# An elementwise add and GELU on one core: row-blocked arrays in place of column slices

## The chip, the core and the metric

The kernel runs on one core of one Trainium2 chip. The metric is the device time of one execution in microseconds (us), as the median of several runs. Beside the runs there is one profiled execution, whose span is the time from its first to its last instruction.

## The reference

```python
x, y: float32 arrays of 1024 x 4096            # 16.78 MB each
z = x + y
out = 0.5 * z * (1 + tanh(sqrt(2 / pi) * (z + 0.044715 * z ** 3)))   # float32
```

Every element of the output depends on the same element of x and of y alone, so the 4,194,304 elements may be handled in any order and any grouping. 33.55 MB are read and 16.78 MB are written.

## The kernel before

**Layout.** Each array is seen as 128 partitions of 32,768 float32 values ("columns" below). Partition p holds 8 consecutive rows of the array, 128 KB in HBM. A load or a store takes a range of columns, so it moves 128 stretches whose starts lie 128 KB apart.

**Buffers.** The tile `zt` (128 x 32768) receives x, then holds the sum z, then the result. y goes through two buffers of 8192 columns. The scratch tiles `wt[c]` lie in PSUM, two of them (`PS = 2`), 2048 columns each.

**Work.** The columns are cut into 16 chunks of 2048. Each chunk c has four steps:

- `add(c)` (L149): z = x + y, in place in `zt`. It runs on DVE for chunks 0, 2, 4, 6, 8 and 12 (`by_dve`), and on POOL for the others.
- `mag(c)` (L154): ACT writes |z| to the PSUM scratch. Because there are two scratch tiles, it needs `end(c - 2)`.
- `gelu(c)` (L157): ACT computes the tanh form of GELU of -|z|, in place in the scratch.
- `end(c)` (L166): DVE adds max(z, 0) to the scratch and writes the result over z.

**Order.** Four queues are written out by hand, and each engine works through its own in order. POOL has its adds in order of chunks, ACT has mag and gelu of each chunk in order, and DVE has all ends in order, with its adds put in between: `by_dve = {0: 0, 2: 0, ...}` says that the add of chunk 2 stands ahead of `end(0)`, and so on. SyncE (SP) issues all transfers, on one queue: y0 (8192 columns), x0 (16384), y1 (8192), x1 (16384), y2, y3 (8192 each), and the stores of 16384, 10240 and 6144 columns. SP waits, in its order, for what a transfer needs: y2 and y3 for the adds that free their buffer, a store for the ends of its columns. The first store waits in addition for the first half of `end(8)` (`FIRST = 8`), so that it joins the queue as the last load nears its end. The functions `begin_early` and `wait_late` move the first two transfers ahead of the program's opening barrier and the last wait behind its closing one; neither is changed.

Of the kernel before, what the change touches and what calls it, by code (L numbers as in the profile page):

```python
# [8 lines left out]
def begin_early(nc, count):  # L9


    head, body = (b.instructions for b in nc.main_func.blocks[:2])
    SP = mybir.EngineType.SP
    moved = [i for i in body if i.engine == SP and isinstance(i, mybir.InstDMACopy)][:count]
    assert not any(i.sync_info and i.sync_info.on_wait for i in moved)
    assert all(i.regs_accessed() == ((), ()) for i in moved)
    at = next(k for k, i in enumerate(head) if i.engine == SP)
    for k, i in enumerate(moved):
        body.remove(i)
        head.insert(at + k, i)  # L20


def wait_late(nc):

    body, end = (b.instructions for b in nc.main_func.blocks[1:3])
    last = [i for i in body if isinstance(i, mybir.InstDMACopy)][-1]
    (sem,) = [u.id for u in last.sync_info.on_update]
    all_done = end[0]  # L30
    reset = next(i for i in end if isinstance(i, mybir.InstDrain) and i.is_reset_sema)
    at = end.index(reset)
    clear = end[at + 1]
    first, stop = reset.reset_range_start, reset.reset_range_stop
    assert all_done.engine == mybir.EngineType.SP and reset.engine == mybir.EngineType.Pool
    assert isinstance(clear, mybir.InstISA) and clear.engine == mybir.EngineType.Pool
    waits = all_done.sync_info.on_wait
    (its,) = [w for w in waits if w.id == sem]

    end[0] = mybir.InstDrain(  # L40
        name=all_done.name, engine=all_done.engine, debug=all_done.debug, is_reset_sema=False,
        sync_info=mybir.SyncInfo(on_wait=[w for w in waits if w.id != sem], on_update=[]),
    )
    parts = []
    for f, e in ((first, sem), (sem + 1, stop)):
        if f < e:
            nc.gpsimd.sem_clear(range(f, e))
            parts.append(nc.cur_bb.bb.instructions.pop())
    end[at + 1 : at + 2] = parts
    end.append(  # L50
        mybir.InstEventSemaphore(
            name=clear.name, engine=mybir.EngineType.Activation, debug=clear.debug,
            sync_info=mybir.SyncInfo(
                on_wait=[its],
                on_update=[
                    mybir.SyncUpdate(
                        sync_type="semaphore", id=sem, ant_name=its.ant_name,
                        update_mode="sem-sub-imm", update_value=its.wait_value,
                    )
                ],  # L60
            ),
        )
    )


@with_exitstack
def kernel(
    ctx: ExitStack,
    tc: tile.TileContext,
    x: bass.AP,  # L70
    y: bass.AP,
    out: bass.AP,
):

    nc = tc.nc
    P = nc.NUM_PARTITIONS
    fp32 = mybir.dt.float32
    act = mybir.ActivationFunctionType
    alu = mybir.AluOpType

    N, D = x.shape
    assert N % P == 0
    TOT = N // P * D  # L90
    xv, yv, ov = (a.rearrange("(p n) d -> p (n d)", p=P) for a in (x, y, out))

    YS = 8192
    CH = 2048
    PS = 2
    xloads = [16384, 16384]
    yloads = [8192, 8192, 8192, 8192]
    FIRST = 8
    stores = [16384, 10240, 6144]

    def ranges(sizes):
        ends = [sum(sizes[: i + 1]) for i in range(len(sizes))]
        assert ends[-1] == TOT
        return [(e - f, e) for e, f in zip(ends, sizes)]

    xr, yr, sr, cr = (ranges(r) for r in (xloads, yloads, stores, [CH] * (TOT // CH)))
    C = len(cr)

    by_dve = {0: 0, 2: 0, 4: 2, 6: 4, 8: 8, 12: 10}

    def over(rs, lo, hi):
        return [i for i, (a, b) in enumerate(rs) if a < hi and b > lo]

    pool_sb = ctx.enter_context(tc.tile_pool(name="xz", bufs=1))
    pool_y = ctx.enter_context(tc.tile_pool(name="y", bufs=2))
    pool_w = ctx.enter_context(
        tc.tile_pool(name="w", bufs=PS, space=bass.MemoryType.PSUM)
    )

    zt = pool_sb.tile([P, TOT], fp32, tag="z", name="z")  # L120
    yt, wt, ends = {}, {}, {}

    def load_x(i):
        a, b = xr[i]
        nc.sync.dma_start(out=zt[:, a:b], in_=xv[:, a:b])

    def load_y(i):
        a, b = yr[i]
        s, o = divmod(a, YS)
        if o == 0:  # L130
            yt[s] = pool_y.tile([P, YS], fp32, tag="y", name=f"y{s}")
        nc.sync.dma_start(out=yt[s][:, o : o + b - a], in_=yv[:, a:b])  # L132

    def store(i):
        a, b = sr[i]
        ins = nc.sync.dma_start(out=ov[:, a:b], in_=zt[:, a:b])
        if i == 0:
            tc.add_manual_dep(
                ins.ins,
                ends[FIRST].name,  # L140
                mybir.DependencyInfo(mybir.DependencyClass.Sync, mybir.DependencyReason.DATA),
                reason="the stores join the queue when the last load is nearly done",
            )

    def add(c):
        a, b = cr[c]
        s, o = divmod(a, YS)
        eng = nc.vector if c in by_dve else nc.gpsimd
        eng.tensor_add(out=zt[:, a:b], in0=zt[:, a:b], in1=yt[s][:, o : o + b - a])  # L149

    def mag(c):
        a, b = cr[c]
        wt[c] = pool_w.tile([P, CH], fp32, tag="w", name=f"w{c}")
        nc.scalar.activation(out=wt[c], in_=zt[:, a:b], func=act.Abs)  # L154

    def gelu(c):
        nc.scalar.activation(  # L157
            out=wt[c], in_=wt[c], func=act.Gelu_apprx_tanh, scale=-1.0
        )

    def end(c):
        a, b = cr[c]
        parts = 2 if c == FIRST else 1
        n = (b - a) // parts
        for o in range(0, b - a, n):
            ins = nc.vector.scalar_tensor_tensor(  # L166
                out=zt[:, a + o : a + o + n], in0=zt[:, a + o : a + o + n], scalar=0.0,
                in1=wt[c][:, o : o + n], op0=alu.max, op1=alu.add,
            )
            ends.setdefault(c, ins.ins)  # L170


    sp = [(load_y, 0), (load_x, 0), (load_y, 1), (load_x, 1), (load_y, 2), (load_y, 3)]
    sp += [(store, i) for i in range(len(stores))]
    pool = [(add, c) for c in range(C) if c not in by_dve]
    dve, acts = [], []
    for c in range(C):
        dve += [(add, k) for k in sorted(by_dve) if by_dve[k] == c] + [(end, c)]
        acts += [(mag, c), (gelu, c)]

    needs = {
        load_x: lambda i: [],
        load_y: lambda i: [
            (add, c) for c in over(cr, yr[i][0] - 2 * YS, yr[i][1] - 2 * YS)
        ],
        add: lambda c: [(load_x, i) for i in over(xr, *cr[c])]
        + [(load_y, i) for i in over(yr, *cr[c])],
        mag: lambda c: [(add, c)] + ([(end, c - PS)] if c >= PS else []),
        gelu: lambda c: [(mag, c)],
        end: lambda c: [(gelu, c)],  # L190
        store: lambda i: [(end, c) for c in over(cr, *sr[i])] + [(end, FIRST)],
    }
    queues = [sp, pool, acts, dve]
    done = set()
    with tc.manual_schedule():
        one = pool_sb.tile([P, 1], fp32, tag="one", name="one")
        nc.vector.memset(one, 0.0)  # L197
        nc.scalar.activation(out=one, in_=one, func=act.Gelu_apprx_tanh)  # L198
        while any(queues):
            moved = False  # L200
            for q in queues:
                while q and all(n in done for n in needs[q[0][0]](q[0][1])):
                    fn, arg = q.pop(0)
                    fn(arg)
                    done.add((fn, arg))
                    moved = True
                    if q is not sp:
                        break
            assert moved, [q[:1] for q in queues]

    ctx.close()
    tc.close()
    tc.compile()  # L213
    begin_early(nc, 2)
    wait_late(nc)
# [30 lines left out]
```

## Time and profile before

| What | Value |
|---|---|
| median of 3 runs | 120.19 us (120.07 to 120.65) |
| profiled execution: span (its time outside the span is not recorded) | 118.57 us |
| bytes moved | 50.33 MB |
| DVE busy | 59.8 us, 50% |
| ACT busy | 60.8 us, 51% |
| POOL busy | 55.5 us, 47% |
| DMA queue, packet time as a share of 16 engines' span | 98.6% |
| TensorE | not used; granted clock 1.00 |

The three computing engines are each busy for about half of the span, and the 16 DMA engines for nearly all of it. "Busy" includes the time in which an instruction has been started but is held up, so a long duration isn't always work. "Landing" of a transfer is the moment at which its semaphore is complete.

### The profile page before, as it was taken

What the parts mean: (1) busy time and instruction counts of PE and PEld (TensorE: products, weight loads), DVE (VectorE), ACT (ScalarE), POOL (GpSimd) and SP (SyncE); (2) the same over time, 40 slices, a digit from 0 to 9 for tenths busy, and PEclk for the clock granted to TensorE, in tenths of its full rate; (3) what the DMA queues carried; (4) which work ended last, traced back from release to release, by engine and by line L of the source; (5) the groups of instructions that cost most, each with busy time, mean ns of one, the idle gap of its engine ahead of it and who ended that gap; (6) DMA issues with size and microseconds to landing.
All of it is one profiled execution on the core that took longest, in us unless ns stands there. A gap on an engine that the chain in (4) does not pass through costs nothing.

```text
span 118.6 us, 160 instructions
## 1 busy us (share of the span) xinstructions
DVE 59.8 (50%) x24; ACT 60.8 (51%) x34; POOL 55.5 (47%) x14
## 2 busy tenths in 40 slices
DVE  0000000000399999699994594257999457742000
ACT  5000000000067979999379705797798999940000
POOL 0000000000399999997000029999999999100000
DMA  7989888998889988988899898998899889999996
GB/s 243 464 365 696 354 354 354 663 398 354 354 387 497 531 354 354 707 354 354 354 420 464 365 520 354 531 531 354 354 531 531 354 354 442 442 442 442 398 398 265
DMA packets 1296, 50.33 MB, mean 424 GB/s; under 512 B 144, under 2 KB 144, under 8 KB 144
## 3 DMA queue, kind: packets, MB, share of 16 engines
q1 hardware_dynamic: 1296, 50.33, 98.6%
HBM read 33.55 MB, written 16.78 MB: 424 GB/s over the span
## 4 chain that ended last, share of the span: by engine, by line
DMA 48%; POOL 34%; POOLq 4%; ACT 3%; DVE 2%; issue 0%; SPq 0%; DVEq 0%
POOL z L149 34%; DMA z<-in_x_dram 26%; DMA y<-in_y_dram 21%; POOLq L213 4%; DVE z L166 2%; ACT w L154 2%; ACT w L157 2%; SPq L132 0%; POOLq L149 0%; DVEq L166 0%
## 5 line engine op out<-in xcount | busy, mean ns | idle before, releaser
L149 POOL TENSOR_TENSOR z<-z,y 128x2048 f32<-128x2048 f32 x10 | 55.3, 5563 | 45.6 <-DMA z<-in_x_dram 31.1
L154 ACT ACTIVATE w<-z 128x2048 f32<-128x2048 f32 x16 | 30.1, 1880 | 42.5 <-DVE z L149 36.0
L166 DVE SCALAR_TENSOR_TENSOR z<-z,w 128x2048 f32<-128x2048 f32 (+1 forms) x17 | 36.4, 2157 | 16.0 <-ACT w L157 16.0
L149 DVE TENSOR_TENSOR z<-z,y 128x2048 f32<-128x2048 f32 x6 | 24.0, 4009 | 30.3 <-DMA z<-in_x_dram 30.1
L157 ACT ACTIVATE w<-w 128x2048 f32<-128x2048 f32 x16 | 29.8, 1862 | 0.5
L198 ACT ACT_TABLE_LOAD x1 | 1.3, 1283 | 1.3 <-PEq L230 1.3
L197 DVE MEMSET one<- 128x1 f32 x1 | 0.1, 59 | 1.3 <-PEq L230 1.3
L198 ACT ACTIVATE one<-one 128x1 f32<-128x1 f32 x1 | 0.2, 203 | 0.0
L230 POOL MEMSET const-float32-0.0<- 128x1 f32 x1 | 0.1, 98 | 0.2 <-issue 0.2
L230 POOL MEMSET const-bfloat16-1.0<- 128x1 bf16 x1 | 0.1, 101 | 0.0
L230 POOL MEMSET const-uint8-127<- 128x1 uint8 x1 | 0.1, 101 | 0.0
L230 POOL MEMSET const-float32-1.0<- 128x1 f32 x1 | 0.1, 98 | 0.0
## 6 DMA issues: line engine op xcount, KB each, us to landing
y<-in_y_dram SPq DMA_DIRECT2D x4, 4096.0 KB, 23.7
out_dram<-z SPq DMA_DIRECT2D x1, 5120.0 KB, 14.9
out_dram<-z SPq DMA_DIRECT2D x1, 3072.0 KB, 11.0
z<-in_x_dram SPq DMA_DIRECT2D x2, 44.9
out_dram<-z SPq DMA_DIRECT2D x1, 21.6
```

The costliest lines, as they stand in the source:

```text
L149: eng.tensor_add(out=zt[:, a:b], in0=zt[:, a:b], in1=yt[s][:, o : o + b - a])
L154: nc.scalar.activation(out=wt[c], in_=zt[:, a:b], func=act.Abs)
L157: nc.scalar.activation(out=wt[c], in_=wt[c], func=act.Gelu_apprx_tanh, scale=-1.0)
L166: ins = nc.vector.scalar_tensor_tensor(out=zt[:, a + o : a + o + n], in0=zt[:, a + o : a + o + n], scalar=0.0, in1=wt[c][:, o : o + n], op ...
L197: nc.vector.memset(one, 0.0)
L198: nc.scalar.activation(out=one, in_=one, func=act.Gelu_apprx_tanh)
L213: tc.compile()
L230: nc = _bacc.Bacc("TRN2", target_bir_lowering=False, num_devices=1)
```

## The change

Each array is now seen as three blocks of 128 consecutive stretches of the flat array: block 0 has 10560 columns (41.25 KB per partition), block 1 has 11968 (46.75 KB), block 2 has 10240 (40 KB). Within a block the 128 stretches follow each other in HBM without a gap. There is one load of x and one of y for each block and one store for each block, nine transfers as before.

SP's order becomes y0, x0, x1, y1, x2, y2, store 0, store 1, store 2. The y blocks share one buffer of 20416 columns: y0 stands at its end, y1 at its beginning (overlapping the first 2112 columns of y0), y2 at its end again (overlapping all of y0 but its first 320 columns, and the last 1792 columns of y1). So y1 waits for the adds of chunks 0 and 1, and y2 for all adds of block 0 and for the add of the one piece of block 1 that lies under it, which is therefore handled first (chunk 6).

There are 18 chunks: six of 1760 columns in block 0; one of 1808 and five of 2032 in block 1 (chunks 6 to 11); and 1024, four times 2048 and 1024 in block 2 (chunks 12 to 17). DVE does the adds of chunks 0, 2, 4, 6, 8, 10, 12, 13 and 15, POOL the others. The built program has DVE's order from the middle of block 1 on as: add 10, end 8, end 9, end 10, add 12, add 13, end 11, end 12, add 15, end 13, end 14, end 15, end 16, end 17. POOL has add 11, add 14, add 16, add 17. The first store waits for `end(9)` instead of the first half of `end(8)`, and no end is split.

```diff
-    YS = 8192
-    CH = 2048
+    BLOCKS = [10560, 11968, 10240]
+    YT = 20416
+    yo = [YT - 10560, 0, YT - 10240]
     PS = 2
-    xloads = [16384, 16384]
-    yloads = [8192, 8192, 8192, 8192]
-    FIRST = 8
-    stores = [16384, 10240, 6144]
+    FIRST = 9
...
+    inside = [[1760] * 6, [2032] * 5 + [1808], [1024] + [2048] * 4 + [1024]]
+    order = [range(6), [5, 0, 1, 2, 3, 4], range(6)]
...
+    def block(flat, i):
+        a, b = br[i]
+        return flat[P * a : P * b].rearrange("(p n) -> p n", p=P)
...
-    by_dve = {0: 0, 2: 0, 4: 2, 6: 4, 8: 8, 12: 10}
+    by_dve = {0: 0, 2: 0, 4: 2, 6: 6, 8: 6, 10: 8, 12: 11, 13: 11, 15: 13}
...
     def load_x(i):
-        a, b = xr[i]
-        nc.sync.dma_start(out=zt[:, a:b], in_=xv[:, a:b])
+        a, b = br[i]
+        nc.sync.dma_start(out=zt[:, a:b], in_=block(xf, i))
...
     def load_y(i):
-        a, b = yr[i]
-        s, o = divmod(a, YS)
-        if o == 0:
-            yt[s] = pool_y.tile([P, YS], fp32, tag="y", name=f"y{s}")
-        nc.sync.dma_start(out=yt[s][:, o : o + b - a], in_=yv[:, a:b])
+        a, b = br[i]
+        nc.sync.dma_start(out=yt[:, yo[i] : yo[i] + b - a], in_=block(yf, i))
...
-    sp = [(load_y, 0), (load_x, 0), (load_y, 1), (load_x, 1), (load_y, 2), (load_y, 3)]
-    sp += [(store, i) for i in range(len(stores))]
+    sp = [(load_y, 0), (load_x, 0), (load_x, 1), (load_y, 1), (load_x, 2), (load_y, 2)]
+    sp += [(store, i) for i in range(len(br))]
...
     needs = {
...
-        store: lambda i: [(end, c) for c in over(cr, *sr[i])] + [(end, FIRST)],
+        store: lambda i: [(end, c) for c in over(cr, *br[i])] + [(end, FIRST)],
     }
```

## The prediction, made before the changed kernel ran

> **What bounds the kernel now.** I read the page first, then the busy time by stretches, then the transfers from issue to landing, then the timeline near the loads' landings and at the end. The page:
>
> ```profile
> span 118.6 us, 160 instructions
> DMA  7989888998889988988899898998899889999996
> q1 hardware_dynamic: 1296, 50.33, 98.6%
> ```
>
> The queue never runs dry. Three stretches (columns: us, busy time of DVE, ACT and POOL, clock, DMA share, GB/s):
>
> ```profile
> 0.00:1.00 1.00, 0.00 (x0) 0.00 (x0) 0.20 (x4) 1.00 0.00 0
> 2.00:30.00 28.00, 0.00 (x0) 0.74 (x2) 0.00 (x0) 1.00 1.00 431
> 79.00:98.00 19.00, 14.09 (x6) 16.91 (x10) 19.00 (x5) 1.00 1.02 442
> ```
>
> Loads and stores move at about 431 to 442 GB/s (packets are counted whole, hence shares above 1), and the queue needs 1 us after the first issue before a byte moves. So the kernel ends when 50.33 MB have gone through, as long as SP always has a transfer in the queue. The engines matter only where they make SP late. Here is how SP stands at the end, and what holds the engines:
>
> ```profile
> 31.45 8.80 DVE L149 TENSOR_TENSOR z<-z,y 128x2048 f32<-128x2048 f32 x2 [30.06 <-DMA z<-in_x_dram]
> 31.49 6.61 POOL L149 TENSOR_TENSOR z<-z,y 128x2048 f32<-128x2048 f32 x1 [31.06 <-DMA z<-in_x_dram]
> ...
> 70.23 2.29 DVE L149 TENSOR_TENSOR z<-z,y 128x2048 f32<-128x2048 f32 x1 [0.28 <-DMA y<-in_y_dram]
> ...
> 81.33 4.50 POOL L149 TENSOR_TENSOR z<-z,y 128x2048 f32<-128x2048 f32 x1
> 83.00 4.98 DVE L149 TENSOR_TENSOR z<-z,y 128x2048 f32<-128x2048 f32 x1
> ...
> 93.90 1.88 ACT L154 ACTIVATE w<-z 128x2048 f32<-128x2048 f32 x1
> 95.81 1.86 ACT L157 ACTIVATE w<-w 128x2048 f32<-128x2048 f32 x1
> 97.58 1.88 ACT L154 ACTIVATE w<-z 128x2048 f32<-128x2048 f32 x1
> ...
> 107.56 0.33 SPq L136 DMA_DIRECT2D out_dram<-z  x1
> ```
>
> An add on DVE takes 2.29 us alone, one on POOL 4.50 (started every 4.47). When both start together, DVE goes first and POOL's lasts 6.61, 2.1 longer. DVE's second add, right behind its first, then waits for POOL's: two take 8.80 = 2.2 + 4.4 + 2.2. At 83.00 a DVE add waits until POOL's running add ends at 85.83 (4.98). So the adds of the two engines exclude each other, and **whoever asks first goes next**. ACT needs 3.68 us for a chunk (93.90 to 97.58) when nothing holds it.
>
> The third store goes out at 107.56 and lands 11.0 us later:
>
> ```profile
> out_dram<-z SPq DMA_DIRECT2D x1, 5120.0 KB, 14.9
> out_dram<-z SPq DMA_DIRECT2D x1, 3072.0 KB, 11.0
> ```
>
> The second, issued at 96.34, lands at 96.34 + 14.9 = 111.2. So the third stands in the queue 3.7 us before the second lands; that is the cover the change has to keep.
>
> **The transfers after.** The chain of waits has x0 landing at 31.35, and the last y load, issued at 57.94, lands 21.9 us later, at 79.84. Between them 40960 columns pass in 48.49 us: 1.184 ns per column. The bytes, the number of transfers (9) and of packets do not change, so I cost the new layout at nothing in the rate; a lower rate is a rival below. Landings after: y0 and x0 (21120 columns) at 31.35 - 3456 x 1.184 ns = 27.26; x1 41.43; y1 55.60; x2 67.72; y2 79.84, exactly as the last load before. With a full queue the stores land 12.50, 14.17 and 12.12 us later: 92.34, 106.51, 118.63.
>
> Would wide spacing of the stretches in HBM have cost something that goes now? The stores, whose stretches lie 128 KB apart too, need 38.7 us for 32768 columns (79.84 to 118.56), 1.182 ns each: loads and stores run at one steady rate, with nothing in it that looks like a collision, so I take no gain. The Trainium skill (DMA: Bandwidth & Descriptors, Latency and other measured facts) reports rates that fall with the row pitch, from 207 GB/s at 512 KiB to half of that at 4 MiB, and come back with a few KiB of padding, which would speak for the change; but its list starts at 512 KiB, and this trace shows no loss at 128 KiB. The same page (Where 436 GB/s comes from) has a ceiling of 435 GB/s, by which 50.33 MB need 115.7 us, so no layout could save more than about 1 us of data time.
>
> **SP's waits.** y1 waits for add 0 (DVE) and add 1 (POOL) after 27.3: 1.9 + 3.8 = 5.7 us for 1760 columns (1760/2048 of the rows), so it is issued near 33, 8 us before x1 lands; x2 is queued behind it on SP and follows at once. y2 waits for add 6, near 57.8, 10 us before x2 lands. Both cost nothing; without that cover each would cost its lateness in full. Store 0 waits for end 9. I follow the chain from y1's landing (columns scaled from the 2048 rows): add 6 on DVE at 55.7 holds off add 7 to 57.6 to 62.0; add 8 on DVE 62.0 to 64.1; add 9 on POOL 64.1 to 68.5; DVE, after ends 6 and 7 (2.0 + 2.2 from 64.1), asks for add 10 at 68.3, 0.25 before POOL asks for add 11, and gets it to 70.6; ends 8, 9 and 10 follow ACT's pairs and end at about 73, 76 and 79.5. Store 0 is issued at 76, 3.8 before y2 lands (before: 77.61, 2.2 before the last load's landing, without a gap), so it costs nothing.
>
> **The tail.** This is the part that costs. Before, the last load's 8192 columns were chunks 12 to 15, and the last store only 6144 columns. Now 10240 columns come with the last load and all are in the last store, and on DVE adds 12 and 13 stand ahead of end 11:
> - 79.9: adds 12 (DVE, 1024 columns) and 14 (POOL) are released by the same landing. DVE first, as at 31.45 and 70.23, holding for 1.1: to 81.0.
> - POOL's add 14 has asked meanwhile: 81.0 to 85.5. DVE's add 13 waits, as its second add did at 31.45: 85.5 to 87.7.
> - end 11 stands behind it on DVE although its gelu was done near 81: 87.6 to 89.9. SP issues store 1 at 89.9, 2.4 before store 0 lands: just in time.
> - mag 13 needs end 11 for its scratch tile, so ACT, idle since gelu 12 at 83.2, starts at 89.9. Chunks 13 to 16 are four times 3.68: to 104.6. No add holds it up (add 15 is through by 94.3, mag 15 comes at 97.3).
> - mag 17 and gelu 17 (half size) end at 106.7, but DVE is later: gelu 16 ends near 104.7, end 16 takes 2.27 and end 17 1.22 (the half-size row's mean): 108.2.
> - SP issues store 2 at **108.3**. By then the queue is dry: store 1 lands at 106.5.
>
> **A cold transfer.** The only one in the trace is the first: y0, 8192 columns, landed 12.0 us after its issue at 0.00 where the rate gives 9.70, so 2.3 us more. At least 1.0 is certain from the first stretch above; a store may start better than the very first load of the program, so I take 2.0, near the only row, and keep 1.0 to 2.3. The last landing is 108.3 + 2.0 + 12.12 = 122.4 (121.4 to 122.7) against 118.57: **+3.85 us**. The Trainium skill (the same page, Latency and other measured facts) gives 0.6 us to the first byte of such a transfer; the row shows none in the first 1.0, and by the page's value the sum would be 121.0.
>
> The median of the runs, 120.19, is 1.62 above the profiled span; I take this as lying around the span and unchanged. Forecast: 120.19 + 3.85 = 124.0.
>
> **Rivals.**
> - *Not slower: the lock passes otherwise.* If DVE takes adds 12 and 13 one after the other and POOL waits for both, end 11 is done 4.5 us (POOL's add) earlier and store 2 goes out at 103.8, 2.7 before store 1 lands: no gap, 118.6, and the median stays at 120.2 (119.8 to 120.6). It decides from about 104.5 (106.5 less a 2.0 cold start): every us that the tail saves up to there is a us of time. For it: DVE issues the two back to back. Against it: the 8.80 us pair at 31.45 is the same situation, and POOL came in between.
> - *Slower still: POOL goes first.* If DVE is not free when y2 lands (I have end 10 done only 0.3 before), POOL's add 14 goes first, add 16 follows add 12, and end 11 comes 4.5 later: 128.5. The same happens if POOL gets add 11 ahead of add 10 (0.25 apart). Every duration in that chain is steady within 0.03 us, which makes it improbable.
> - *The new layout moves at another rate.* One per cent less costs the loads 0.8 and the last store 0.1 on top of the forecast: 124.9; a better first start could give back a part of the 2.3 us that y0 lost, of which I allow 0.3. Nothing in the trace measures either; I keep -0.3 to +1.
>
> **Chances.** The forecast 0.82; lock otherwise 0.07; POOL first 0.06; the rate off by more than 1% 0.05. What a measurement can tell from no change is about 0.5%, 0.6 us. The forecast's own range is 122.9 (cold start 1.0) to 124.4 (2.3) from the start-up alone, with the chain's 0.3 and the rate's 1 us: 122.4 to 125.2, which already holds 8 in 10. Only the first rival is not slower, and in most of it nothing can be measured: faster 0.02, same 0.06, slower 0.92.
>
> **What would show it.** In the profile after: last load landing at 79.8; the adds at 79.9 as DVE 1.2, POOL about 5.6, DVE's second ending near 87.8; an ACT idle of about 6.7 us that a DVE end on the scratch tile ends at 89.9; the third store issued at 108.3; two slices near 106.5 to 109.5 with little DMA; the queue's share near 95%. I am wrong if the third store is issued before 105, if the DMA row stays full to the end, or if the loads land at another time than 79.8.

## The result and the profile after

The changed kernel takes 124.46 us (median of 5 runs, 124.10 to 124.49) against 120.19 us in the same session: 1.0343 times the time before, 95% interval 1.0323 to 1.0362. The forecast was 124.0. The profiled execution has a span of 122.58 us against 118.57.

The page of the changed kernel:

```profile
span 122.6 us, 172 instructions
DMA  7999999999799979999999999999997999259994
q1 hardware_dynamic: 1296, 50.33, 95.7%
```

Bytes and packets are as before, but the queue's share falls from 98.6% to 95.7%, and the DMA row has a hole of two slices (2 and 5 tenths) four slices before the end. The busy time by stretches (us, busy time of DVE, ACT and POOL, clock, DMA share, GB/s) shows it in detail:

```profile
104.00:106.00 2.00, 0.54 (x2) 2.00 (x2) 0.00 (x0) 1.00 0.67 287
106.00:107.00 1.00, 1.00 (x1) 0.97 (x2) 0.00 (x0) 1.00 0.00 0
107.00:108.00 1.00, 1.00 (x2) 0.47 (x1) 0.00 (x0) 1.00 0.00 0
108.00:109.00 1.00, 1.00 (x1) 0.00 (x0) 0.00 (x0) 1.00 0.00 0
```

No packet starts from 106 to 109 (the share counts a packet whole, where it starts), while DVE is busy throughout. By the packet records the last packet of store 1 ends at 106.96 and the first of store 2 starts at 109.88, so the queue is empty for 2.9 us. The timeline from the last load's landing on says what the queue waits for:

```profile
80.74 7.73 DVE L165 TENSOR_TENSOR z<-z,y 128x1024 f32<-128x1024 f32 x2 [0.55 <-DMA y<-in_y_dram]
80.78 16.44 POOL L165 TENSOR_TENSOR z<-z,y 128x2048 f32<-128x2048 f32 x3 [5.09 <-DMA y<-in_y_dram]
...
88.39 3.39 DVE L180 SCALAR_TENSOR_TENSOR z<-z,w 128x2032 f32<-128x2032 f32 x2
90.68 1.88 ACT L170 ACTIVATE w<-z 128x2048 f32<-128x2048 f32 x1 [6.62 <-DVE z L180]
...
109.05 0.33 SPq L152 DMA_DIRECT2D out_dram<-z  x1
```

DVE's adds 12 and 13 take 7.73 us together, because POOL's add 14 comes between them. In a narrower window (85 to 86) the same view has adds 14 and 13 each by itself:

```profile
80.78 5.54 POOL L165 TENSOR_TENSOR z<-z,y 128x2048 f32<-128x2048 f32 x1 [5.09 <-DMA y<-in_y_dram]
81.88 6.59 DVE L165 TENSOR_TENSOR z<-z,y 128x2048 f32<-128x2048 f32 x1
```

Add 13 has been started at 81.88, but it ends only 2.2 us after POOL's add 14 (86.32). End 11, which stands behind it, runs from 88.39 to 90.65; ACT has been idle for 6.62 us until that end frees its scratch tile. From there ACT's pairs of mag and gelu run without a pause worth naming, and the last store is issued at 109.05. In the view of the transfers from issue to landing, the three stores need

```profile
DMA to landing us min/median/max: 13.5/16.6/16.6
```

so store 1 (issued at 90.67) lands at 107.3 and store 2 at 109.05 + 13.5 = 122.55, within 0.03 us of the end of the span.

Two lines of the chain of waits (start, us) give the loads' landings:

```profile
0.42 27.51 DMA z<-in_x_dram
...
58.46 22.19 DMA y<-in_y_dram
```

x0 lands at 27.93 (I had 27.26) and the last load at 80.65 (79.84). Those forecasts were counted from x0's line in the kernel before, 31.35:

```profile
0.43 30.92 DMA z<-in_x_dram
```

### The profile page after: what moved, and what is told of

Its sections match the earlier page's. It is cut to its first block, busy times and chain, and to the rows that moved or that the text cites. A ratio compares the mean times of both kernels' runs of the same rounds, so it can differ in the third digit from the quotient of the medians.

```text
span 122.6 us, 172 instructions
## 1 busy us (share of the span) xinstructions
DVE 67.4 (55%) x28; ACT 61.1 (50%) x38; POOL 53.0 (43%) x13
## 3 DMA queue, kind: packets, MB, share of 16 engines
q1 hardware_dynamic: 1296, 50.33, 95.7%
## 4 chain that ended last, share of the span: by engine, by line
DMA 59%; ACT 10%; issue 8%; DVE 6%; POOL 5%; DVEq 1%; SPq 0%; POOLq 0%
DMA y<-in_y_dram 36%; DMA z<-in_x_dram 22%; ACT w L170 6%; POOL z L165 5%; ACT w L174 4%; DVE z L180 3%; DVE z L165 2%; DVEq L231 1%; SPq L148 0%; DVEq L165 0%; DVEq L180 0%; POOLq L165 0%
## 5 line engine op out<-in xcount | busy, mean ns | idle before, releaser
L165 POOL TENSOR_TENSOR z<-z,y 128x1760 f32<-128x1760 f32 (+3 forms) x9 | 52.7, 5886 | 44.0 <-DMA z<-in_x_dram 27.6
L170 ACT ACTIVATE w<-z 128x1760 f32<-128x1760 f32 (+4 forms) x18 | 30.4, 1689 | 44.5 <-DVE z L165 35.7
L165 DVE TENSOR_TENSOR z<-z,y 128x1760 f32<-128x1760 f32 (+4 forms) x9 | 31.5, 3531 | 31.0 <-DMA z<-in_x_dram 26.7
L180 DVE SCALAR_TENSOR_TENSOR z<-z,w 128x1760 f32<-128x1760 f32 (+4 forms) x18 | 36.5, 2043 | 9.3 <-ACT w L174 9.3
L174 ACT ACTIVATE w<-w 128x1760 f32<-128x1760 f32 (+4 forms) x18 | 30.1, 1672 | 0.6
```

The source lines that it names most:

```text
L165: eng.tensor_add(out=zt[:, a:b], in0=zt[:, a:b], in1=yt[:, o:e])
L170: nc.scalar.activation(out=wt[c][:, : b - a], in_=zt[:, a:b], func=act.Abs)
L174: nc.scalar.activation(out=wt[c][:, :n], in_=wt[c][:, :n], func=act.Gelu_apprx_tanh, scale=-1.0)
L180: ins = nc.vector.scalar_tensor_tensor(out=zt[:, a:b], in0=zt[:, a:b], scalar=0.0, in1=wt[c][:, : b - a], op0=alu.max, op1=alu.add,)
```

## Experiments

The theory: the tail decides. The last store's 10240 columns are not ready when the queue runs dry, because of the order of adds on DVE, the turns that DVE's and POOL's adds take, and the size of that store. The main rival: the row blocks, or the transfers cut from them, are slower as such. All kernels are the changed kernel with the edit shown, unless it says otherwise; medians are compared with the kernel before in the same session (120.05 in the first eight, 120.13 in the last three).

**1. End 11 ahead of add 13.**

```diff
-    by_dve = {0: 0, 2: 0, 4: 2, 6: 6, 8: 6, 10: 8, 12: 11, 13: 11, 15: 13}
+    by_dve = {0: 0, 2: 0, 4: 2, 6: 6, 8: 6, 10: 8, 12: 11, 13: 12, 15: 13}
```

> DVE does end 11 before add 13 (in the changed kernel add 13 stands first); nothing else differs. Theory (the tail's chain of adds and ends makes the last store late): end 11 ends near 84.2 instead of 90.65, store 1 is issued there, and ACT's mag 13 waits for add 13 (88.5) instead of end 11 (90.65). But add 15 then comes a place later against POOL's add 16, and end 13 with it, so the last store is issued only about 0.7 us earlier: 108.3 against 109.05, span 121.9 against 122.55, median 123.8. Rival (the new layout or its transfers are slower as such): no change, 124.4.

Measured: 123.73 us (ratio 1.0295, 1.0262 to 1.0328), span 121.85, last store at 108.32. Its timeline:

```profile
84.14 4.43 DVE L165 TENSOR_TENSOR z<-z,y 128x2048 f32<-128x2048 f32 x1
...
88.60 1.88 ACT L170 ACTIVATE w<-z 128x2048 f32<-128x2048 f32 x1 [4.46 <-DVE z L165]
89.62 5.46 DVE L165 TENSOR_TENSOR z<-z,y 128x2048 f32<-128x2048 f32 x1
...
97.31 1.88 ACT L170 ACTIVATE w<-z 128x2048 f32<-128x2048 f32 x1 [1.25 <-DVE z L180]
```

ACT starts 2.1 us earlier (88.60), and most of it is lost again where add 15 now waits for POOL (5.46 instead of 3.29) and holds end 13. The last store goes out 0.73 us earlier (108.32), as expected, and the time stands 3.7 us above the kernel before instead of 4.3. The intervals of the two times overlap a little, so the issue in the profile is the clearer sign. The order of one instruction matters, and by the amount that the turns of the two engines give.

**2. Adds 13 and 14 change engines.**

```diff
-    by_dve = {0: 0, 2: 0, 4: 2, 6: 6, 8: 6, 10: 8, 12: 11, 13: 11, 15: 13}
+    by_dve = {0: 0, 2: 0, 4: 2, 6: 6, 8: 6, 10: 8, 12: 11, 14: 12, 16: 14}
```

> Adds 13, 15 and 17 go to POOL and adds 14 and 16 to DVE, each behind an end (by_dve 12: 11, 14: 12, 16: 14), so no DVE add stands ahead of end 11 but the small add 12. Theory: end 11 ends near 84.2, mag 13 starts when POOL's add 13 ends, near 86.3 instead of 90.7, the last store is issued near 104.7, 2.6 before store 1 lands (107.3), and the queue has no gap: span 119.4 (118.6 and the 0.8 by which the loads land later than before), median 121.2. Rival (layout or transfers slower as such): 124.4, with the queue as dry as in the changed kernel.

Measured: 121.44 us (1.0099, 1.0064 to 1.0135), span 119.73. Lines of the timeline and of the page:

```profile
86.68 1.88 ACT L170 ACTIVATE w<-z 128x2048 f32<-128x2048 f32 x1 [2.31 <-POOL z L165]
104.97 0.33 SPq L152 DMA_DIRECT2D out_dram<-z  x1
q1 hardware_dynamic: 1296, 50.33, 98.3%
```

ACT starts mag 13 when POOL's add 13 is done, the last store goes out 4.1 us earlier, in time, and the queue's share is back at 98.3%. Same layout, same transfers, other engines for a few adds: against the kernel before of its session, 2.9 of the 4.3 us are gone.

**3. The last store in two halves.**

```diff
+    sr = br[:2] + ranges([5120, 5120], br[2][0])
...
+        a, b = sr[i]
+        k = min(i, 2)
+        s = br[k][0]
+        ins = nc.sync.dma_start(out=block(of, k)[:, a - s : b - s], in_=zt[:, a:b])
...
-        store: lambda i: [(end, c) for c in over(cr, *br[i])] + [(end, FIRST)],
+        store: lambda i: [(end, c) for c in over(cr, *sr[i])] + [(end, FIRST)],
```

> The last store of 10240 columns is cut into two of 5120 (chunks 12 to 14, 15 to 17); engines unchanged, one transfer more. Theory: the first half is issued after end 14 (100.5), 6.8 before store 1 lands at 107.3; it takes 6.06 us, so the queue is fed until 113.3, and the second half, issued at 109.05, stands behind it: no gap, span 119.4, median 121.2. The lateness of the last end costs nothing any more though no engine is faster. Rival (layout or transfers slower as such): 124.4 or a little more for the tenth transfer.

Measured: 121.37 us (1.0097, 1.0067 to 1.0127), span 119.46. SP issues the halves at 100.55 and 109.05, and the stretch that held the hole is full:

```profile
104.00:114.00 10.00, 3.55 (x3) 3.44 (x3) 0.00 (x0) 1.00 0.99 427
```

No engine is faster than in the changed kernel, and the last end comes at the same time, 109.05; only the cover is longer. Experiments 2 and 3 take the hole away in two different ways and end within 0.1 us of each other.

**4. The same blocks in the old layout.**

```diff
-    xf, yf, of = (t.rearrange("n d -> (n d)") for t in (x, y, out))
+    xf, yf, of = (t.rearrange("(p n) d -> p (n d)", p=P) for t in (x, y, out))
...
-        return flat[P * a : P * b].rearrange("(p n) -> p n", p=P)
+        return flat[:, a:b]
```

> The changed kernel with the old layout in HBM (partition p holds 8 consecutive rows; a transfer takes a range of columns, 128 KB apart); block sizes, order, chunks and engines as changed. Theory A (the layout costs the loads 0.8 us at the start, since y0's first packets took 2.0 to 3.1 us instead of 1.2 to 2.1): loads land at 79.85 instead of 80.65, everything behind moves with them, span 121.8, median 123.7. Theory B (the start differs from one program or run to the next, or with the packet size, not with the layout): 124.2 to 124.5, loads landing near 80.5. Rival (the whole slowdown is the layout): 120.2.

Measured: 124.40 us (1.0354, 1.0326 to 1.0382). The row blocks in HBM, the most visible part of the change, do nothing to the time that can be told apart from noise (0.3%). The rival falls, and so does theory A; theory B's 124.2 to 124.5 holds, with the last load landing at 80.33.

**5. The first store later** (`FIRST = 10` for `FIRST = 9`).

> The changed kernel with its first store tied to end 10 instead of end 9: issued near 80.2 instead of 76.6, so that the queue runs dry for some 1.5 us between the last load and the first store. Theory (the end is set by the tail's chain from y2's landing to end 17, the queue has slack there): that gap costs nothing, 124.4; at most it is 0.4 faster, if the last load's packets, of which 8 took 0.1 to 0.4 us longer after 77.5, are no longer slowed by the waiting store. Rival (what counts is the sum of the queue's busy time and its gaps): 1.5 slower, 125.9.

Measured: 124.02 us (1.0328, 1.0313 to 1.0343), span 122.08, first store at 79.85. Between 79 and 80 no data packet starts now:

```profile
79.00:80.00 1.00, 0.82 (x1) 0.97 (x2) 0.00 (x0) 1.00 0.01 0
```

By the packet records the last load's packets end at 79.69 at the latest and the store's first one starts at 80.69, so the queue is empty for 1.0 us. The rival's 125.9 doesn't come: the time is no longer, and this hole costs nothing, because the end is set by the tail's chain. The time is even 0.4 less (0.3 against the kernel before of each session), but the intervals overlap. In the profile the chain starts earlier, since the last load lands at 80.13 instead of 80.65; these are its lines in the chain of waits:

```profile
0.43 27.15 DMA z<-in_x_dram
58.09 22.04 DMA y<-in_y_dram
```

Of this 0.52 us, 0.35 is there at x0 already (27.58 instead of 27.93), long before any store; only the other 0.17 can be the store's.

**6. Experiment 2 in the old layout**, to find the 1.3 to 1.4 us that remain.

> The kernel with adds 13 and 14 swapped (121.4, no gap at store 2) with the old layout, 128 KB apart. It asks whether the 1.3 us that this kernel still stands above the kernel before are the layout's. Theory A (they are the start and the last load's packets beside a waiting store, both without regard to the layout): 121.2 to 121.4. Theory B (row blocks cost the first packets or the turn from loads to stores): 120.1 to 120.4.

Measured: 121.34 us (1.0104, 1.0087 to 1.0121). Not the layout: theory B falls.

**7 and 8. Experiment 2 with the first store earlier or later.** In 7 `FIRST = 8`; in 8 end 10 is done in four parts and the first store tied to the first:

```diff
-    FIRST = 9
+    FIRST = 10
...
+        n = (b - a) // (4 if c == FIRST else 1)
+        for o in range(0, b - a, n):
...
+            ends.setdefault(c, ins.ins)
```

> Adds 13 and 14 swapped, row blocks, and the first store tied to end 8 instead of end 9: it joins the queue near 73.5 instead of 76.2, and so stands behind the last load for 5.5 us instead of 2.8. Theory S (load packets are slowed while a store waits behind them on the same engines, as the last 16 of y2 were, by 0.3 to 1.0 us each): two more packets of each engine are slowed, and the time rises by 0.5 to 1.5 us over 121.4. Rival (a single cost of the turn from loads to stores, or chance): 121.4 unchanged.

> Adds 13 and 14 swapped, row blocks, end 10 done in four parts and the first store tied to the first part: it joins the queue near 78.2 instead of 76.2, about 1 us before the last load leaves the first engines (the kernel before: 77.6, 1.5 before). Theory S (a store that waits behind the load slows its last packets): y2's last packets stay near 1.52 us, the last load lands near 80.0 instead of 81.0, and the whole is 0.5 to 0.9 us faster than 121.4: 120.5 to 120.9. Rival (a single cost of the turn, or chance): 121.4 or, with the queue dry for a moment, more.

Measured: 121.63 us in 7 (1.0137, 1.0115 to 1.0159) and 121.27 in 8 (1.0098, 1.0085 to 1.0111), little apart from 121.44 and from each other. Theory S had 121.9 to 122.9 for 7 and 120.5 to 120.9 for 8; both times miss it and lie where the rival had them. What speaks for theory S is in the profiles alone. The last load's wait (chain of waits) in experiments 2 and 8:

```profile
58.07 22.88 DMA y<-in_y_dram
```

```profile
58.14 22.04 DMA y<-in_y_dram
```

Store 0 goes out at 76.25 in experiment 2 and 78.31 in 8. In 2 the last packet of every engine before the store lasts 0.3 to 1.0 us more than the usual 1.51; in 7, with the store at 73.2, 0.7 to 1.25 more, and 7 packets before them 0.2 to 0.6; in 8 and in 5, where the store comes at 78.3 and 79.85, none. From x0's landing to the last load's it is 53.39 us in 2, 53.66 in 7, 52.54 in 8 and 52.55 in 5. The median span falls from 119.5 in experiment 2 to 119.0 in 8. But in 8 the time outside the span is 2.2 to 2.3 us, where it is 1.9 in experiment 2, and that takes more than half of the gain back.

**9. The kernel before with seven more DVE instructions.**

```diff
-        parts = 2 if c == FIRST else 1
+        parts = 2 if c == FIRST else 8 if c == 2 else 1
```

> The kernel before with end 2 done in eight parts of 256 columns: seven more DVE instructions (as many as the changed kernel has more of on that engine), in a place where DVE has slack. The span must stay at 118.6. Theory L (the time outside the span grows with the length of an engine's program: 1.5 us in the kernel before, 1.9 in the changed kernel with 55 DVE records instead of 48, 2.25 in the one with 58): median 120.45, 0.4 above the kernel before. Rival (what lies around the span differs with the transfers or the order of the tail): 120.05.

Measured: 120.42 us (1.0018, 1.0003 to 1.0032). The group view shows the eight parts, with no idle time before them, and the page the span:

```profile
L166 DVE SCALAR_TENSOR_TENSOR z<-z,w 128x256 f32<-128x256 f32 x8 | 2.7, 406 | 0.0
span 118.7 us, 167 instructions
```

Over all its runs the span is 118.4 to 118.7, that of the kernel before in the same session mostly 118.5 to 118.7; the time outside it is 1.84 to 1.93 us against 1.44 to 1.53. The whole time is 0.3 us longer (0.04 to 0.4 by the interval). So seven more records on DVE (instructions of the engine and of its sequencer, as the profile has them) are enough to add 0.4 us outside what the profile's span shows; the changed kernel, with as many, has 1.86 to 1.93.

Together these account for experiment 2. Its profiled execution (121.66) stands 1.6 us above the kernel before: 0.3 is there at x0 (27.56 against 27.26), 0.8 arises between x0 and the last load (53.39 against 52.58 at the rate of the kernel before), and 0.4 to 0.5 lies outside the span.

**10. Experiment 8 with two parts instead of four.**

```diff
-        n = (b - a) // (4 if c == FIRST else 1)
-        for o in range(0, b - a, n):
+        cuts = [0, 508, b - a] if c == FIRST else [0, b - a]
+        for o, e in zip(cuts, cuts[1:]):
+            n = e - o
```

> As the kernel with its first store tied to a first part of end 10, but end 10 in two parts (508 and 1524 columns) instead of four: two instructions fewer. Span 118.9 as there. Theory L: the time outside the span falls from 2.25 back to 1.9, median 120.8. Rival (it is the later store that costs outside the span): 121.2.

Measured: 121.21 us (1.0089, 1.0066 to 1.0112), 2.2 to 2.3 us outside the span: theory L missed, and the rival's 121.2 came. Yet the later store by itself doesn't cost this, for experiment 5, with its first store later still (79.85), has 1.84 to 1.94 us outside, at 55 records on DVE. With 56 records the time outside is that of 58. Together with experiment 9 the times outside are 1.5, 1.9 and 2.25 us at 48, 55 and 56 or more. They look like steps; but experiments 8 and 10 alone have more than 55 records, and both split end 10, so the cause of the second step stays open.

**11. The kernel before with its first store earlier** (`FIRST = 7` for `FIRST = 8`).

> The kernel before with its first store tied to the first half of end 7 instead of end 8: it joins the queue near 69 instead of 77.6 and stands behind the last load for all of its 10 us. Theory S (load packets are slowed while a store waits behind them): y3's packets get longer, the last ones by 0.4 to 1 us, the loads land 0.5 to 1.5 us later and so does the end: median 120.6 to 121.6. Rival (the turn from loads to stores costs only in the new order of transfers): 120.05.

Measured: 121.19 us (1.0079, 1.0054 to 1.0104), span 119.8. The store goes out at 70.02 instead of 77.61; the last packet of each engine lasts 0.35 to 0.67 us more than 1.21. That is half of the 1.1 us. The spans of all five runs are 119.5 to 119.8, so each has about the whole of it; but in the one profile the other half has arisen before the store was issued (y2 lands at 70.70, 0.56 later than before, after x1 packets that took 0.1 longer), and I can't tie that to the edit.

## Why the prediction was right

The forecast was 3.85 us more; 4.27 were measured, 4.0 of them in the span. The mechanism came as written: the tail makes the last store late and the queue runs dry. Of my signs of being wrong one came up, since the loads didn't land at 79.8 (below). By its steps:

- **The rate.** Costed at nothing; experiments 4 and 6 show it to be nothing within 0.3% (124.40 and 121.34 in the old layout, 124.46 and 121.44 in row blocks).
- **The order of turns between DVE and POOL.** As written: DVE, POOL, DVE, with 7.73 us for adds 12 and 13 (I had 79.9 to 87.7, 7.8), an ACT idle of 6.62 (6.7), and from the adds' start to the last store's issue 28.31 us (28.4). The rival in which DVE takes both adds first didn't come. Nor did the one in which POOL goes first: DVE was idle for 0.55 us when y2 landed, 0.25 more than I had allowed.
- **SP's waits for y1 and y2, and store 0.** The first two were hidden, as predicted. Store 0 at 76.63 was predicted to cost nothing "3.8 before y2 lands": this is the step that was wrong in kind. When a store joined this early, last packets of the load took longer, 8 of 16 by 0.1 to 0.4 us here, and the last load starts the tail's chain. It is a small term: against experiment 5, where no packet is slowed, it is 0.2 us from x0's landing to the last load's (52.71 against 52.55).
- **The landings.** The loads were 0.81 late. 0.67 of it is there at x0, with the first packets; over all kernels with these blocks x0 landed at 27.38 to 27.93, in both layouts, where the rate of the kernel before gives 27.26. It is a start that varies, and no experiment separates its cause. The other 0.14 are the slowed packets. The "better first start" that I allowed 0.3 for didn't come.
- **The cold transfer.** 2.0 was taken, between 1.0 and 2.3. Store 2 landed 13.5 us after its issue, and 12.12 are its columns: 1.4, of which 0.83 pass before its first packet starts. The program's first load, the only row there was, was too dear a model for a later store.
- **Outside the span.** Taken as unchanged at 1.62; it was 1.88, 0.26 more. But 1.62 set the median of the runs against the span of one execution; the runs of the kernel before that list their own span have about 1.5, so the growth is 0.4, as in experiment 9. This term was missing.

So the sum came within 0.5 us because the tail, its largest term, was right to 0.1, and the smaller errors (0.8 for the landings and 0.3 outside the span too little, 0.6 for the cold transfer and 0.1 in the tail too much) partly cancelled: that is luck. The bounds from the start-up alone, 122.9 and 124.4, were each 0.1 off; 121.4 and 122.7 plus 1.62 give 123.0 and 124.3. No version here beats the kernel before: the best of the new order, experiment 10, has a median span 0.4 us longer and 0.7 us more outside it.

## What to carry to other kernels

In a kernel that its DMA queue bounds, count for every transfer how long it stands in the queue before the one ahead lands: that cover, not the engines' busy shares, says whether a reordering costs. A larger last store shortens the cover from both sides: more columns must be computed before it goes out, and fewer bytes lie in the stores that run meanwhile. Cutting it in two gave back 3 us without making any engine faster. And an instruction put ahead of another on an engine that works in order can cost what it waits for, and not only what it takes: add 13 takes 2.2 us, and it held end 11 for 6.5 (81.9 to 88.4).

## What the runs showed of the hardware that was not expected

- A store issued well before the last load has left the queue makes the last packets of that load longer, by 0.1 to 1.25 us each (stores issued at 70.0 to 76.6); issued at 77.6 to 79.9 it doesn't. It isn't enough that the store comes first: in the kernel before it was issued at 77.61, and the last packets, which started 0.25 to 0.54 us after that, took their usual 1.21. The packet durations show this directly; the times of experiments 7 and 8 don't set it apart from noise.
- The time outside the span is not a constant of the chip: 1.5, 1.9 and 2.25 us for programs of 48, 55 and 56 or more records on DVE. Experiment 9 ties the first of these steps to the added instructions; the second is only seen, in experiments 8 and 10.
- Stretches that lie 128 KB apart in HBM, and stretches of 40 to 47 KB that follow each other, are read and written equally fast here (124.40 against 124.46 us, and 121.34 against 121.44).
